# Grouped-query attention on one core: sharing the exponential between ScalarE and VectorE in another pattern, with larger loads

## The chip, the core and the metric

The kernel runs on one core of a Trainium2 chip. The metric is the device time of one execution in microseconds. The engines are named as the profile names them: PE (TensorE matmul; PEld is its weight load), DVE (VectorE), ACT (ScalarE), POOL (GpSimd) and SP (SyncE, which here only issues DMAs). On-chip memory is SBUF; matmuls write PSUM, of which eight banks of 128 x 512 float32 exist in this kernel's tiling.

## What is computed

Eight batches of 512 positions, 32 query heads that share 8 key/value heads in groups of four, 64 values per head. Inputs and output are float32.

```python
batch, seq, n_heads, n_kv_heads, dim = 8, 512, 32, 8, 64
scores = np.einsum('bhqd,bhkd->bhqk', Q, K_expanded) / np.sqrt(dim)
weights = np.exp(scores - np.max(scores, axis=-1, keepdims=True))
weights = weights / (np.sum(weights, axis=-1, keepdims=True) + 1e-10)
output = np.einsum('bhqk,bhkd->bhqd', weights, V_expanded)
```

The order of the 512 keys is free, as long as K and V have the same one: a softmax row sums over all of them.

## The kernel before, in words

The work is cut into 64 jobs; job j is one batch and one key/value head (two jobs make a unit u, eight jobs a batch). A job has four query heads, taken as two head pairs (`i` = 0, 1). Its scores are 16 blocks, each of one head pair, one key chunk `kc` and one head `m` of the pair: 128 keys on the partitions x 512 queries. Each block needs one score matmul, one exponential into `pt` (float16), and its share of the 64 `pv` matmuls (128 x 65: the 65th column of `v` is one, so that the sum of a softmax row comes out beside its values).

Exponentials are made in two ways.

- ACT does two blocks at once: `act_tile` (line 273) has PE write two blocks into a PSUM tile `s_ps` (two buffers of two banks), and ACT reads it and writes `pt` (line 279).
- DVE and POOL do the other blocks of a job by bits: `exp_d` (283) scales the scores to an int16 `u` (290), `exp_d2` (297) takes the low ten bits `f` (301, DVE), makes a factor `g` from it (304, POOL, "the first correction step") and a product `w` (308, POOL), and `exp_d4` (314) adds `w` to `u` (317, DVE), whose bits are the float16 result. `exp_d4` of a job runs in the job behind it.

`WIDE` (line 41) says which jobs give DVE three blocks instead of two: the even jobs from 4 on. A wide job leaves ACT 13 blocks: six tiles of two and one single block, which goes into one bank of the PSUM tile `d_ps` and is made by `act_tile(j, 4, bank)` (called `beside` in the loop). A narrow job leaves ACT 14 blocks, seven tiles. The third block of a wide job is scored and scaled in the job ahead of it (a 128x512 `u`).

Scheduling is by hand: the order of the program is the order on each engine. The loop at line 541 runs the scores and exponentials of job j beside the `pv` matmuls of job j - 1 (`last`). In one turn: tile 0; two score blocks for DVE and their `u`; tile 1; in some jobs a check of V (`check_v`, line 232, DVE); the first 32 `pv` matmuls of `last` in two runs of 16 with tile 2 between them, and `norm` (a reciprocal, line 387, and a product, line 392, both DVE, which read the `pv` tile); tile 3; the single block, if wide; eight transposes of queries for job j + 2 (line 210); `exp_d4(last)`; a check of the sums every eighth job (`check_sums`, line 356, DVE); `exp_d2(j)`; the copy of the transposed queries `qt` (line 214, DVE); then the other 32 `pv` matmuls, cut into three runs by `cut`, with tiles 5 and 6 and the early third block of the next job between them; and `norm` again.

`d_ps` and `pv` have one buffer each of two banks. So the first `pv` matmul of a half waits for the `norm` of the half before it, and new blocks in `d_ps` wait for the `u` and `qt` that read the old ones. In job 61, `norm` also closes the checks (lines 356 and 410 to 413).

Loads are DMAs issued by POOL, which turn float32 into bfloat16 on the way: `load_q` (line 132) one unit of Q, 512 KB as it lands; `load_k` (111) a batch of K; `load_v` (120) a quarter of a batch of V, 128 KB. SP issues the stores and, from `dma_k`, the DMA transposes of K. In the loads `(sc p)` means that a partition holds positions 128 apart.

Of the kernel before, what the change touches and what calls it, by code (L numbers as in the profile page):

```python
# [13 lines left out]
BF16 = mybir.dt.bfloat16  # L14
FP16 = mybir.dt.float16
# [3 lines left out]
ALU = mybir.AluOpType  # L19
# [7 lines left out]
EXP_K = 3.28614867e-04  # L27
EXP_F1 = 1045.05112
# [9 lines left out]
LAST_SUMS = NLAST * 2 * 4  # L38


WIDE = lambda j: j >= 4 and j % 2 == 0


@with_exitstack
# [23 lines left out]
def fast_path(ctx, tc, Q, K, V, out, flag, ident):  # L68
    nc = tc.nc
    B, S, H, D = Q.shape  # L70
    KV = K.shape[2]
    HPG = H // KV
    SC = S // 128
    GP = KV // 2
    NU = B * GP
# [7 lines left out]
    qnat_pool = ctx.enter_context(tc.tile_pool(name="qnat", bufs=4))  # L83
# [20 lines left out]
    vt = [const_pool.tile([128, SC, KV, D + 1], BF16, name=f"v{j}") for j in range(2)]  # L104
# [4 lines left out]
    kn, qn, kt, qt, twice = {}, {}, {}, {}, {}  # L109

    def load_k(b, lo=0, hi=KV):
        if b not in kn:
            kn[b] = knat_pool.tile([128, SC, KV, D], BF16, name="k_nat")
        nc.gpsimd.dma_start(
            out=kn[b][:, :, lo:hi, :],
            in_=K[b, :, lo:hi, :].rearrange("(sc p) g d -> p sc g d", p=128),
        )


    def load_v(b, lo=0, hi=KV, chunks=range(SC)):  # L120
        for sc in chunks:
            nc.gpsimd.dma_start(  # L122
                out=vt[b % 2][:, sc, lo:hi, 0:D],
                in_=V[b, sc * 128:(sc + 1) * 128, lo:hi, :],
            )

    def load_v_head(b, g):
        nc.gpsimd.dma_start(
            out=vt[b % 2][:, :, g, 0:D], in_=V[b, :, g, :].rearrange("(sc p) d -> p sc d", p=128)
        )  # L130

    def load_q(u, lo=0, hi=2 * HPG):
        b, gp = divmod(u, GP)
        h0 = gp * 2 * HPG
        if u not in qn:
            qn[u] = qnat_pool.tile([128, SC, 2 * HPG, D], BF16, name="q_nat")
        nc.gpsimd.dma_start(  # L137
            out=qn[u][:, :, lo:hi, :],
            in_=Q[b, :, h0 + lo:h0 + hi, :].rearrange("(sc p) h d -> p sc h d", p=128),
        )  # L140

# [60 lines left out]
    def trans_q(j, bank, lo=0, hi=NPAIR, other=None):  # L202
        u, g = divmod(j, 2)
        ps = bank.bitcast(BF16).rearrange("p (i sc c) -> p i sc c", i=NPAIR, sc=SC)
        done = []
        for i in range(lo, hi):
            for sc in range(SC):
                h = g * HPG + 2 * i
                done.append(apart(
                    nc.tensor.transpose(ps[:, i, sc, :], qn[u][:, sc, h:h + 2, :], ident), other  # L210
                ))
        if u not in qt:
            qt[u] = qt_pool.tile([128, 2, NPAIR, S], BF16, name="qt")
        return done, lambda: apart(nc.vector.tensor_copy(  # L214
            out=qt[u][:, g, lo:hi, :], in_=ps[:, lo:hi, :, :].rearrange("p i sc c -> p i (sc c)")
        ), other)
# [13 lines left out]
    def check_v(b, sc):  # L230
        n = b * SC + sc
        nc.vector.tensor_reduce(  # L232
            out=okv[:, n:n + 1], in_=vt[b % 2][:, sc, :, 0:D], op=ALU.max, axis=AX.XY,
            apply_absolute_value=True,
        )

    NJOB = NU * 2
    DPAIR = NPAIR - 1  # L240

    def taken(j):
        return 1 if j == NJOB - 1 else 3 if WIDE(j) else 2

# [8 lines left out]
        return [[every[n] for n in group] for group in groups if group]  # L253

    jobs, osb, invs = {}, {}, {}

    def scores(j, ps, i, kc, m):
        u, g = divmod(j, 2)
# [14 lines left out]
    def act_tile(j, n, spare=None):  # L273
        group = act_tiles(j)[n]
        i, kc, lo = group[0]
        ps = s_pool.tile([128, 2, S], FP32, name="s_ps") if spare is None else spare
        for _, _, m in group:
            scores(j, ps[:, m, :], i, kc, m)
        return nc.scalar.activation(  # L279
            out=jobs[j]["pt"][:, i, kc, lo:, :], in_=ps[:, lo:, :], func=EXP, scale=scale  # L280
        )
# [15 lines left out]
    def exp_d2(j, engine=None):  # L297
        st = jobs[j]
        by_bits = engine is None
        engine = engine or nc.gpsimd  # L300
        nc.vector.tensor_single_scalar(  # L301
            out=st["f"], in_=st["u"], scalar=1023, op=ALU.bitwise_and
        )
        engine.tensor_scalar(  # L304
            out=st["g"], in0=st["f"], scalar1=-EXP_F1, scalar2=EXP_K * 2.0 ** (24 * by_bits),
            op0=ALU.add, op1=ALU.mult,
        )
        product = lambda: engine.tensor_tensor(  # L308
            out=st["w"], in0=st["g"], in1=st["f"].bitcast(FP16) if by_bits else st["f"],
            op=ALU.mult,  # L310
        )
        return product() if by_bits else product

    def exp_d4(j):
# [18 lines left out]
    def pv(j, i, lo, hi):  # L333
        st = jobs[j]
        u, g = divmod(j, 2)
        b, gp = divmod(u, GP)
        if lo == 0:

            t = d_tile() if (j, i) == (NJOB - 1, 0) else pv_tile()
            t = t.rearrange("p m (qc c) -> p m qc c", qc=SC)  # L340
            st["pv"][i] = t[:, :, :, 0:D + 1]
        order = blocks(j, i)
        for n in range(lo, hi):
            kc, m, qc = order[n]
            nc.tensor.matmul(  # L345
                st["pv"][i][:, m, qc, :],
                st["pt"][:, i, kc, m, qc * 128:(qc + 1) * 128],
                vt[b % 2][:, kc, 2 * gp + g, :],
                start=(n < 2 * SC and qc == 0),
                stop=(n >= len(order) - 2 * SC and qc == SC - 1),  # L350
            )
# [11 lines left out]
    def check_sums():  # L363
        while full:
            k, n = full.pop()
            cols = n * 2 * SC
            flat = invs.pop(k).rearrange("p s m qc -> p (s m qc)")[:, 0:cols]
            in_bounds((ok[:, 0:cols], ok[:, 0:cols]), flat, ok[:, 0:cols])
# [83 lines left out]
    first_q = Q[0, :, 0:2, :].rearrange("(sc p) h d -> p sc h d", p=128)  # L452

    def key_head(g, queue, part=slice(0, SC)):
        of = K[0, :, g, :].rearrange("(sc p) d -> p sc d", p=128)
        queue.dma_start(out=kf[g][:, part, :], in_=of[:, part, :])

    for queue, part in zip((nc.sync, nc.scalar), parts):
# [8 lines left out]
    for j in range(2):  # L467
        nc.gpsimd.memset(vt[j][:, :, :, D:D + 1], 1.0)
    load_k(0, 2, 4)
    load_q(1)  # L470
    load_v_head(0, 1)
    load_k(0, 4, KV)
    load_v(0, 2, KV)
    nc.gpsimd.memset(ones, 1.0)
    nc.gpsimd.memset(ok, 1.0)

# [17 lines left out]
    for sc in range(SC):  # L494
        n, at = divmod(sc, half)
# [13 lines left out]
    ps = s_tile()  # L509
# [31 lines left out]
    for j in range(1, NJOB - 1):  # L541
        last = j - 1
        u, g = divmod(j, 2)
        b, gp = divmod(u, GP)
        open_job(j)
        if j == 1:

            nc.gpsimd.tensor_copy(out=gate, in_=jobs[0]["pt"][0:1, 0, SC - 1, 0, 0:1])
            load_q(2)
            load_q(3)  # L550
        if g == 0 and u >= 1 and u + 3 < NU:
            load_q(u + 3)
        if (gp, g) == (1, 0) and b + 1 < B:
            load_k(b + 1)
        if 3 <= 2 * gp + g < 3 + SC and b + 1 < B:
            load_v(b + 1, chunks=(2 * gp + g - 3,))
        if j == 1:
            dma_k(0, 2)
        if gp == 2 and g == 0 and b + 1 < B:
            dma_k(b + 1)  # L560

        cut = (4, 18) if taken(j) > 2 else (11, 19)
        act_tile(j, 0)
        if j == 1:
            piece(1, *first_k(1, 0, bank[:, 1, S // 2:]))
        exp_d(j, 0, 2, d_tile())()
        act_tile(j, 1)

        if j == 8:
            check_v(0, 0)  # L570
        if g == 1 and 1 < j and b < B - 1:
            check_v(b, gp)
        if 0 <= j - 8 * (B - 1) < SC:
            check_v(B - 1, j - 8 * (B - 1))
        pv(last, 0, 0, 16)
        act_tile(j, 2)
        pv(last, 0, 16, 32)
        norm(last, 0)
        act_tile(j, 3)

        reads = []
        bank = d_tile()
        beside = act_tile(j, 4, bank) if taken(j) > 2 else None

        ahead = (j + 1,) if j < 2 else (3, 4) if j == 2 else (j + 2,)
        for n, to in enumerate(ahead):
            if to < NJOB:
                reads.append(trans_q(to, bank[:, n, :], other=beside)[1])
        if j == 1:
            reads.append(first_k(1, 1, bank[:, 1, :])[1])  # L590
        exp_d4(last)
        check_sums()
        exp_d2(j)
        copies = [read() for read in reads]
        if taken(j) == 2:
            act_tile(j, 4)
        pv(last, 1, 0, cut[0])
        act_tile(j, 5)
        if taken(j + 1) > 2:
            exp_d(j + 1, 2, taken(j + 1), bank[:, 1:2, :], copies[0])()  # L600
        pv(last, 1, *cut)
        act_tile(j, 6)
        pv(last, 1, cut[1], 32)
        norm(last, 1)
        del jobs[last]
# [146 lines left out]
```

## Time and profile before

| what | value |
| --- | --- |
| time, median of 3 runs | 411.88 us (411.63 to 411.93) |
| time of the profiled execution | 411.81 us |
| its span in the trace | 410.0 us |
| DVE busy | 342.0 us, 608 instructions |
| POOL busy | 306.1 us, 216 instructions |
| DMA packets | 93310, 67.74 MB, mean 165 GB/s |
| HBM read, written | 50.33 MB, 33.55 MB |

A group of instructions is one line of the kernel, one engine and one shape; its row has the busy time, the mean duration of one in ns, and the idle time of the engine ahead of it with what ended that. Timeline rows have the start in us, the duration, and the instruction; neighbours that are alike are merged (x16). Instructions of one engine overlap at their ends: the next one starts before the recorded end of the one ahead of it, so that what an instruction costs in a busy queue is the distance from its start to the next start (or from end to end), which is less than its duration.

### The profile page before, as it was taken

To read this page: it belongs to the slowest core of one execution; us is meant where nothing else is said; L and a number is where in the kernel's file an instruction comes from. 1 tells how busy PE (TensorE), PEld (TensorE's weight loads), DVE (VectorE), ACT (ScalarE), POOL (GpSimd) and SP (SyncE) were. 2 spreads that over 40 slices of the span, in tenths; PEclk is the share of its full clock that TensorE was granted. 3 is DMA by queue.
4 is the path that set the end of the run, shared out by engine and by line. 5 is a ranking of instruction groups with operands and counts; after the bars stand their busy time and mean duration, and the time that the engine had idled before them with its cause. 6 is when DMAs were issued, how large, how long until landed. Compare 5 with 4: busy or idle time off the path is not lost.

```text
span 410.0 us, 13056 instructions
## 1 busy us (share of the span) xinstructions
PE 377.9 (92%) x5670; PEld 233.1 (57%) x5670; DVE 342.0 (83%) x608; ACT 401.2 (98%) x455; POOL 306.1 (75%) x216
## 2 busy tenths in 40 slices
PE   7999999999999999999999999999999999999985
PEld 3565555555555555555655655555555555655553
DVE  4787898888898888888888888888889888998775
ACT  5999999999999999999999999999999999999995
POOL 9868767878679777688777897587776887676562
PEclk9999999999999999999999999999999999999999
DMA  9999984999939995499984999669996799752205
GB/s 145 161 211 190 207 167 134 197 139 198 189 109 227 130 275 116 108 208 127 227 221 79 208 185 213 157 85 213 170 205 156 130 205 199 152 143 104 104 19 195
DMA packets 93310, 67.74 MB, mean 165 GB/s; under 512 B 53312, under 2 KB 76352, under 8 KB 93248
## 3 DMA queue, kind: packets, MB, share of 16 engines
q0 software_dynamic: 55488, 24.91, 52.9%
q1 hardware_dynamic: 37216, 41.75, 36.8%
q8 instruction: 45, 0.74, 0.7%
q10 hardware_dynamic: 544, 0.20, 0.2%
q14 instruction: 17, 0.14, 0.1%
HBM read 50.33 MB, written 33.55 MB: 205 GB/s over the span
## 4 chain that ended last, share of the span: by engine, by line
ACT 79%; PE 12%; DVE 6%; issue 2%; ACTq 0%; DVEq 0%
ACT pt L279 79%; PE s_ps L261 7%; PE pv L345 4%; DVE pt L317 1%; DVE o_sb L392 1%; DVE qt L214 1%; PE s_ps L481 1%; DVE u L290 1%; DVE ok L356 1%; DVE inv L387 0%; PE d_ps L261 0%; DVE f L301 0%; ACTq L279 0%; DVE inv_last L387 0%; PE d_ps L345 0%
## 5 line engine op out<-in xcount | busy, mean ns | idle before, releaser
L279 ACT ACTIVATE pt<-s_ps 128x1024 f16<-128x1024 f32 x418 | 394.7, 1256 | 0.2 <-PE s_ps L261 0.2
L345 PEld LDWEIGHTS <-pt 128*128 128x128 f16 x4096 | 142.1, 98 | 75.7 <-issue 55.6
L345 PE MATMUL pv<-v,pt 128*128 128x65 bf16 x4064 | 179.3, 195 | 1.0 <-DVE o_sb L392 0.7
L261 PE MATMUL s_ps<-qt,kt 64*128 64x512 bf16 x781 | 153.2, 383 | 23.4 <-ACT pt L279 17.0
L308 POOL TENSOR_TENSOR w<-g,f 128x1024 bf16<-128x1024 bf16 (+1 forms) x63 | 163.1, 2588 | 5.3
L304 POOL TENSOR_SCALAR g<-f 128x1024 bf16<-128x1024 int16 (+1 forms) x63 | 78.4, 1244 | 90.6 <-DVE f L301 90.5
L290 DVE TENSOR_SCALAR u<-d_ps 128x1024 int16<-128x1024 f32 (+1 forms) x94 | 97.5, 1037 | 0.0
L261 PEld LDWEIGHTS <-kt 64*128 64x128 bf16 x960 | 55.3, 93 | 66.3 <-issue 37.0
L392 DVE TENSOR_TENSOR o_sb<-pv,inv 128x512 f32<-128x512 f32 x121 | 83.6, 691 | 4.2
L387 DVE RECIPROCAL inv<-pv 128x8 f32<-128x8 f32 x121 | 25.1, 207 | 49.8 <-PE pv L345 49.8
L317 DVE TENSOR_TENSOR pt<-u,w 128x1536 uint16<-128x1536 int16 (+1 forms) x64 | 51.4, 802 | 0.3 <-POOL w L308 0.2
L261 PE MATMUL d_ps<-qt,kt 64*128 64x512 bf16 x179 | 46.1, 375 | 0.1
L214 DVE COPY qt<-d_ps 128x1024 bf16<-128x1024 bf16 x62 | 42.2, 682 | 0.0
L210 PEld LDWEIGHTS <-q_nat 128*128 128x128 bf16 x508 | 28.5, 98 | 20.2 <-issue 20.2
L210 PE MATMUL d_ps<-ident,q_nat 128*128 128x128 bf16 x496 | 38.3, 220 | 0.0
L301 DVE TENSOR_SCALAR f<-u 128x1536 int16<-128x1536 int16 (+1 forms) x64 | 30.7, 480 | 0.0
L122 POOL DMA_DIRECT2D v<-in_V_dram x32 | 29.0, 913 | 0.0
L137 POOL DMA_DIRECT2D q_nat<-in_Q_dram x33 | 27.0, 819 | 0.1
L279 ACT ACTIVATE pt<-d_ps 128x512 f16<-128x512 f32 x30 | 25.9, 863 | 0.0
L232 DVE TENSOR_REDUCE okv<-v 128x1 f32<-128x512 bf16 x32 | 21.6, 675 | 0.0
L261 PE MATMUL s_ps<-qt,kt_first 64*128 64x512 bf16 x56 | 11.1, 399 | 1.7 <-ACT pt L279 1.5
L261 PEld LDWEIGHTS <-kt_first 64*128 64x128 bf16 x64 | 3.9, 94 | 5.6 <-issue 3.0
(57 smaller groups left out, 49.1 us busy)
## 6 DMA issues: line engine op xcount, KB each, us to landing
out_dram<-o_sb SPq DMA_DIRECT2D x31, 1024.0 KB, 7.3
q_nat<-in_Q_dram POOLq DMA_DIRECT2D x31, 512.0 KB, 6.2
k_nat<-in_K_dram POOLq DMA_DIRECT2D x7, 512.0 KB, 8.7
v<-in_V_dram POOLq DMA_DIRECT2D x28, 128.0 KB, 7.4
kt<-kt SPq DMA_DIRECT2D x14, 256.0 KB, 4.4
out_dram<-o_sb SPq DMA_DIRECT2D x4, 256.0 KB, 2.3
kt<-k_nat SPq DMA_TRANSPOSE x32, 6.5
v<-in_V_dram POOLq DMA_DIRECT2D x4, 96.0 KB, 7.6
```

The costliest lines, as they stand in the source:

```text
L122: nc.gpsimd.dma_start(out=vt[b % 2][:, sc, lo:hi, 0:D], in_=V[b, sc * 128:(sc + 1) * 128, lo:hi, :],)
L210: nc.tensor.transpose(ps[:, i, sc, :], qn[u][:, sc, h:h + 2, :], ident), other
L214: return done, lambda: apart(nc.vector.tensor_copy(out=qt[u][:, g, lo:hi, :], in_=ps[:, lo:hi, :, :].rearrange("p i sc c -> p i (sc c)")), ...
L261: return nc.tensor.matmul(ps, keys[64 * m:64 * m + 64, g if u == 0 else g ^ m, kc * 128:(kc + 1) * 128], qt[u][64 * m:64 * m + 64, g, i, : ...
L279: return nc.scalar.activation(out=jobs[j]["pt"][:, i, kc, lo:, :], in_=ps[:, lo:, :], func=EXP, scale=scale)
L290: return lambda: nc.vector.tensor_scalar(out=st["u"][:, lo:hi, :], in0=ps[:, 0:hi - lo, :], scalar1=A_U, scalar2=B_U, op0=ALU.mult, op1=AL ...
L301: nc.vector.tensor_single_scalar(out=st["f"], in_=st["u"], scalar=1023, op=ALU.bitwise_and)
L304: engine.tensor_scalar(out=st["g"], in0=st["f"], scalar1=-EXP_F1, scalar2=EXP_K * 2.0 ** (24 * by_bits), op0=ALU.add, op1=ALU.mult,)
L308: product = lambda: engine.tensor_tensor(out=st["w"], in0=st["g"], in1=st["f"].bitcast(FP16) if by_bits else st["f"], op=ALU.mult,)
L317: nc.vector.tensor_tensor(out=st["pt"][:, DPAIR, :, :, :].rearrange("p kc m q -> p (kc m) q")[:, d_block(j):d_block(j) + n, :].bitcast(U16 ...
L345: nc.tensor.matmul(st["pv"][i][:, m, qc, :], st["pt"][:, i, kc, m, qc * 128:(qc + 1) * 128], vt[b % 2][:, kc, 2 * gp + g, :], start=(n < 2 ...
L392: nc.vector.tensor_tensor(out=osb[u][:, :, h:h + 2, :].rearrange("p qc m d -> p m qc d"), in0=sums[:, :, :, 0:D], in1=inv[:, :, :, None].t ...
```

## The change

`WIDE` becomes three jobs of four: from job 4 on, all but those with j % 4 == 3. In a wide job behind a wide one (j % 4 is 1 or 2) the factor `g` is made by DVE and not by POOL. Where the job behind is wide too (j % 4 is 1), `g` and `w` come later in the program: behind the `u` of the next job's third block. `check_sums` and `check_v` move to between tile 1 and the first `pv` matmuls. In wide jobs the second run of `pv` matmuls moves to before the early block, and `cut` has a third form. K and V are read as `(p sc)`: a partition holds four neighbouring positions. V is loaded a batch at a time, Q two units at a time (the tile has twice the heads), in jobs that a table names.

```diff
-WIDE = lambda j: j >= 4 and j % 2 == 0
+WIDE = lambda j: j >= 4 and j % 4 < 3
...
-    def load_v(b, lo=0, hi=KV, chunks=range(SC)):
-        for sc in chunks:
+    def load_v(b, lo=0):
+        to = vt[b % 2][:, :, lo:, 0:D]
+        of = V[b, :, lo:, :].rearrange("(p sc) g d -> p sc g d", p=128)
+        if lo:
+            for sc in range(SC):
+                nc.gpsimd.dma_start(out=to[:, sc], in_=of[:, sc])
+        else:
             nc.gpsimd.dma_start(
-                out=vt[b % 2][:, sc, lo:hi, 0:D],
-                in_=V[b, sc * 128:(sc + 1) * 128, lo:hi, :],
+                out=to.rearrange("p sc g d -> p (sc g) d"),
+                in_=of.rearrange("p sc g d -> p (sc g) d"),
             )
...
+    def load_q(p, lo=0, hi=4 * HPG):
+        b, at = divmod(p, GP // 2)
+        h0 = at * 4 * HPG
...
+    CHECKS = {}
+    for b in range(B):
+        span = range(max(3, 8 * b + 1), min(8 * b + 9, NJOB - 3))
+        two = [j for j in span if not WIDE(j)]
+        odd = [j for j in span if WIDE(j) and not WIDE(j + 1)]
+        at = [(j, 0) for j in two + odd] + [(j, 1) for j in two]
+        at += [(j, 0) for j in span if j not in two + odd]
+        CHECKS.update(zip(at, [(b, sc) for sc in range(SC)]))
+
+    def in_jobs(load, first, jobs):
+        for n, j in enumerate(jobs):
+            LOADS.setdefault(j, []).append((load, first + n))
+
+    LOADS = {1: [(load_q, 1, 0, 2 * HPG), (load_q, 1, 2 * HPG, 4 * HPG)]}
+    in_jobs(load_k, 1, [3] + [8 * b for b in range(1, B - 1)])
+    in_jobs(load_q, 2, [3, 7, 8] + [8 * b + n for b in range(1, B) for n in (3, 7)][:2 * B - 5])
+    in_jobs(load_v, 1, [8 * b + 4 for b in range(B - 1)])
...
+        odd = WIDE(j) and WIDE(j - 1)
         nc.vector.tensor_single_scalar(
             out=st["f"], in_=st["u"], scalar=1023, op=ALU.bitwise_and
         )
-        engine.tensor_scalar(
-            out=st["g"], in0=st["f"], scalar1=-EXP_F1, scalar2=EXP_K * 2.0 ** (24 * by_bits),
-            op0=ALU.add, op1=ALU.mult,
-        )
...
+        def factor():
+            (nc.vector if odd else engine).tensor_scalar(
+                out=st["g"], in0=st["f"], scalar1=-EXP_F1,
+                scalar2=EXP_K * 2.0 ** (24 * by_bits), op0=ALU.add, op1=ALU.mult,
+            )
...
+        if odd and WIDE(j + 1):
+            return lambda: (factor(), product())
+        factor()
         return product() if by_bits else product
...
-        cut = (4, 18) if taken(j) > 2 else (11, 19)
+        cut = (11, 19) if taken(j) < 3 else (4, 18) if taken(last) < 3 else (4, 16)
...
+        if j < 4 or j % 4 == 0:
+            check_sums()
+        if (j, 0) in CHECKS:
+            check_v(*CHECKS[j, 0])
         pv(last, 0, 0, 16)
...
         exp_d4(last)
-        check_sums()
-        exp_d2(j)
+        rest = exp_d2(j)
...
         act_tile(j, 5)
+        if beside:
+            pv(last, 1, *cut)
         if taken(j + 1) > 2:
             exp_d(j + 1, 2, taken(j + 1), bank[:, 1:2, :], copies[0])()
-        pv(last, 1, *cut)
+        if rest:
+            rest()
+        if (j, 1) in CHECKS:
+            check_v(*CHECKS[j, 1])
+        if not beside:
+            pv(last, 1, *cut)
```

More of the change, by code (lines that the diff above doesn't have):

```diff
@@ L115, in load_k @@
             out=kn[b][:, :, lo:hi, :],
-            in_=K[b, :, lo:hi, :].rearrange("(sc p) g d -> p sc g d", p=128),
+            in_=K[b, :, lo:hi, :].rearrange("(p sc) g d -> p sc g d", p=128),
         )
-    def load_v(b, lo=0, hi=KV, chunks=range(SC)):
-        for sc in chunks:
+    def load_v(b, lo=0):
[5 more added lines that the diff above has]
+        else:
             nc.gpsimd.dma_start(
-                out=vt[b % 2][:, sc, lo:hi, 0:D],
-                in_=V[b, sc * 128:(sc + 1) * 128, lo:hi, :],
+                out=to.rearrange("p sc g d -> p (sc g) d"),
+                in_=of.rearrange("p sc g d -> p (sc g) d"),
             )
@@ L128, in load_v_head @@
         nc.gpsimd.dma_start(
-            out=vt[b % 2][:, :, g, 0:D], in_=V[b, :, g, :].rearrange("(sc p) d -> p sc d", p=128)
+            out=vt[b % 2][:, :, g, 0:D], in_=V[b, :, g, :].rearrange("(p sc) d -> p sc d", p=128)
         )
[L132 to L136, printed above, removed]
+    def load_q(p, lo=0, hi=4 * HPG):
+        b, at = divmod(p, GP // 2)
+        h0 = at * 4 * HPG
+        if p not in qn:
+            qn[p] = qnat_pool.tile([128, SC, 4 * HPG, D], BF16, name="q_nat")
         nc.gpsimd.dma_start(
-            out=qn[u][:, :, lo:hi, :],
+            out=qn[p][:, :, lo:hi, :],
             in_=Q[b, :, h0 + lo:h0 + hi, :].rearrange("(sc p) h d -> p sc h d", p=128),
@@ L207, in trans_q @@
             for sc in range(SC):
-                h = g * HPG + 2 * i
+                h = (u % 2) * 2 * HPG + g * HPG + 2 * i
                 done.append(apart(
-                    nc.tensor.transpose(ps[:, i, sc, :], qn[u][:, sc, h:h + 2, :], ident), other
+                    nc.tensor.transpose(ps[:, i, sc, :], qn[u // 2][:, sc, h:h + 2, :], ident),
+                    other,
                 ))
@@ L303, in exp_d2, with product @@
         )
-        engine.tensor_scalar(
-            out=st["g"], in0=st["f"], scalar1=-EXP_F1, scalar2=EXP_K * 2.0 ** (24 * by_bits),
-            op0=ALU.add, op1=ALU.mult,
-        )
[L308 to L311, printed above, removed]
+        def factor():
[3 more added lines that the diff above has]
+            )
+        def product():
+            engine.tensor_tensor(
+                out=st["w"], in0=st["g"], in1=st["f"].bitcast(FP16) if by_bits else st["f"],
+                op=ALU.mult,
+            )
+        if odd and WIDE(j + 1):
+            return lambda: (factor(), product())
+        factor()
         return product() if by_bits else product
@@ L454, in key_head @@
     def key_head(g, queue, part=slice(0, SC)):
-        of = K[0, :, g, :].rearrange("(sc p) d -> p sc d", p=128)
+        of = K[0, :, g, :].rearrange("(p sc) d -> p sc d", p=128)
         queue.dma_start(out=kf[g][:, part, :], in_=of[:, part, :])
@@ L469, in fast_path @@
     load_k(0, 2, 4)
-    load_q(1)
+    load_k(0, 4, KV)
+    load_q(0, 8, 16)
     load_v_head(0, 1)
-    load_k(0, 4, KV)
-    load_v(0, 2, KV)
+    load_v(0, 2)
     nc.gpsimd.memset(ones, 1.0)
@@ L548, in fast_path @@
             nc.gpsimd.tensor_copy(out=gate, in_=jobs[0]["pt"][0:1, 0, SC - 1, 0, 0:1])
[L549 to L556, printed above, removed]
+        for load, *of in LOADS.get(j, ()):
+            load(*of)
         if j == 1:
@@ L567, in fast_path @@
         act_tile(j, 1)
[L569 to L574, printed above, removed]
+        if j < 4 or j % 4 == 0:
+            check_sums()
+        if (j, 0) in CHECKS:
+            check_v(*CHECKS[j, 0])
         pv(last, 0, 0, 16)
```

## The prediction

> **What bounds the kernel now.** I read the busy times first, then ACT's timeline in the middle of the run, then PE's and DVE's over the same two jobs.
>
> ```profile
> span 410.0 us, 13056 instructions
> PE 377.9 (92%) x5670; PEld 233.1 (57%) x5670; DVE 342.0 (83%) x608; ACT 401.2 (98%) x455; POOL 306.1 (75%) x216
> ```
>
> ACT is busy for 98% of the span. The next fence is its timeline; its last row is the first tile after ACT had waited, from the start of the run.
>
> ```profile
> 209.25 0.91 ACT L279 ACTIVATE pt<-d_ps 128x512 f16<-128x512 f32 x1
> 209.73 12.35 ACT L279 ACTIVATE pt<-s_ps 128x1024 f16<-128x1024 f32 x13
> 221.67 0.90 ACT L279 ACTIVATE pt<-d_ps 128x512 f16<-128x512 f32 x1
> ...
> 9.17 1.02 ACT L279 ACTIVATE pt<-s_ps 128x1024 f16<-128x1024 f32 x1 [0.18 <-PE s_ps L261]
> ```
>
> Rows overlap, so I count from end to end. The single blocks end at 210.16 and 222.57, the 13 tiles between them at 222.08: a tile costs 11.92 / 13 = 0.917 us and a single block 0.49, with no gap. A wide job is 6 x 0.917 + 0.49 = 5.99 us of ACT, a narrow one 6.42. So ACT sets the pace, and a block taken from it is worth 0.917 - 0.49 = 0.427 us while nothing else is late.
>
> How late may something else be? PE, over one wide job (from 205.14) and the start of the next:
>
> ```profile
> 205.14 0.39 PE L261 MATMUL s_ps<-qt,kt 64*128 64x512 bf16 x2
> 206.05 0.39 PE L261 MATMUL s_ps<-qt,kt 64*128 64x512 bf16 x2 [0.31 <-ACT pt L279]
> 206.38 0.67 PE L345 MATMUL pv<-v,pt 128*128 128x65 bf16 x16
> 206.98 0.39 PE L261 MATMUL s_ps<-qt,kt 64*128 64x512 bf16 x2
> 207.30 0.67 PE L345 MATMUL pv<-v,pt 128*128 128x65 bf16 x16
> 207.90 0.39 PE L261 MATMUL s_ps<-qt,kt 64*128 64x512 bf16 x2
> 208.13 0.38 PE L261 MATMUL d_ps<-qt,kt 64*128 64x512 bf16 x1
> 209.23 0.39 PE L261 MATMUL s_ps<-qt,kt 64*128 64x512 bf16 x2
> 210.09 0.39 PE L261 MATMUL s_ps<-qt,kt 64*128 64x512 bf16 x2
> 211.13 0.39 PE L261 MATMUL s_ps<-qt,kt 64*128 64x512 bf16 x2
> 212.04 0.39 PE L261 MATMUL s_ps<-qt,kt 64*128 64x512 bf16 x2 [0.31 <-ACT pt L279]
> 212.37 0.67 PE L345 MATMUL pv<-v,pt 128*128 128x65 bf16 x16
> 212.97 0.39 PE L261 MATMUL s_ps<-qt,kt 64*128 64x512 bf16 x2
> ```
>
> Pairs of score matmuls come 0.92 apart because a tile's buffer is free only when ACT has ended the tile two before it. Sixteen `pv` matmuls fill such a slot (206.38 to 206.98 is 0.60, and 0.33 for the pair), so PE can catch up little: 0.31 in the slot behind the job's first pair. From the free buffer to the end of its tile the least is a hand-over of some 0.06, the pair's 0.39, again 0.06, and 1.02 in ACT, in all 1.53; ACT's pace allows 2 x 0.917 = 1.83. **A pair may be 0.30 us late before ACT stands still**, and what is beyond that is lost for good.
>
> **What the change takes from ACT.** Wide jobs go from 30 (even, 4 to 62) to 45 (three in each four, 4 to 62): 15 x 0.427 = 6.4 us less. PE's work does not change in sum.
>
> **What it puts on DVE.** I call the jobs of a group 4n to 4n+3. DVE's rows in which each instruction starts right behind the other give its costs from start to start:
>
> ```profile
> 208.00 0.21 DVE L387 RECIPROCAL inv<-pv 128x8 f32<-128x8 f32 x1 [0.80 <-PE pv L345]
> 209.46 0.55 DVE L301 TENSOR_SCALAR f<-u 128x1536 int16<-128x1536 int16 x1
> 209.92 0.68 DVE L214 COPY qt<-d_ps 128x1024 bf16<-128x1024 bf16 x1
> 213.03 0.67 DVE L232 TENSOR_REDUCE okv<-v 128x1 f32<-128x512 bf16 x1
> 213.99 0.21 DVE L387 RECIPROCAL inv<-pv 128x8 f32<-128x8 f32 x1 [0.28 <-PE pv L345]
> 214.23 0.69 DVE L392 TENSOR_TENSOR o_sb<-pv,inv 128x512 f32<-128x512 f32 x1
> 214.84 0.95 DVE L317 TENSOR_TENSOR pt<-u,w 128x1536 uint16<-128x1536 int16 x1
> 215.70 0.61 DVE L356 SCALAR_TENSOR_TENSOR ok<-inv,ok 128x128 f32<-128x128 f32 x2
> 217.17 0.68 DVE L290 TENSOR_SCALAR u<-d_ps 128x512 int16<-128x512 f32 x1
> 217.77 0.19 DVE L387 RECIPROCAL inv<-pv 128x8 f32<-128x8 f32 x1
> 218.00 0.69 DVE L392 TENSOR_TENSOR o_sb<-pv,inv 128x512 f32<-128x512 f32 x1
> ```
>
> The new instruction is `g` at 128x1536 on DVE; it ran there once, at 512:
>
> ```profile
> L304 DVE TENSOR_SCALAR g<-f 128x512 bf16<-128x512 int16 x1 | 0.3, 295 | 0.0
> L301 DVE TENSOR_SCALAR f<-u 128x512 int16<-128x512 int16 x1 | 0.3, 287 | 0.0
> L304 POOL TENSOR_SCALAR g<-f 128x1536 bf16<-128x1536 int16 x30 | 44.0, 1467 | 50.0 <-DVE f L301 50.0
> L308 POOL TENSOR_TENSOR w<-g,f 128x1536 bf16<-128x1536 bf16 x30 | 92.9, 3096 | 2.5
> L317 DVE TENSOR_TENSOR pt<-u,w 128x1536 uint16<-128x1536 int16 x30 | 28.5, 949 | 0.2 <-POOL w L308 0.2
> ```
>
> `f` grows from 0.287 at 512 to 0.55 at 1536, so I take 0.56 for `g`, some 0.47 from start to start as `f` has (209.46 to 209.92 is 0.46). Its bounds are 0.30 (the row at 512) and 0.95 (the sum `pt` of the same length); it stands near `f` because the two are 8 ns apart at 512.
>
> Now the chain that matters: the second `norm` of a job frees `pv` for the next job's first run. In 4n+1, from the first reciprocal: reciprocal 0.24, `norm` 0.61, `pt` 0.86, `f` 0.46, `qt` 0.60, `u` of the next job's third block 0.60, `g` 0.47, reciprocal 0.23, `norm` 0.69, hand-over 0.06, in all 4.82. Each part is one of the distances above (`qt` has the length of that `u`). The reciprocal itself waits for PE and comes 2.86 into a wide job (208.00 - 205.14). So `pv` is free 7.68 after the start of 4n+1, which is 1.69 into 4n+2; the first run stands at 1.24 there now (212.37 - 211.13). It is 0.45 late, and so is the pair behind it (212.97 now). Less 0.30, **ACT stands still for 0.15 us in each job 4n+2**. In 14 of the 15 (6 to 58) that is 2.1 us.
>
> In 4n+2 the reciprocal comes at 1.69 + 1.62 = 3.31, `g` needs the whole of `f` right ahead of it (0.55 + 0.03, the gap between 213.99 + 0.21 and 214.23), and there is no third block to scale: 4.34 to the next free `pv`, 0.27 late in 4n+3. That is inside the 0.30, with 0.03 to spare. Jobs 4n+3 (narrow, 6.42) and 4n (no `g`, the narrow 128x1024 `pt`) bring DVE back to where it waits for PE.
>
> The 15th is job 62. Job 61 is narrow now and closes the checks between `norm` and `pt`:
>
> ```profile
> 388.52 0.49 DVE L356 SCALAR_TENSOR_TENSOR ok<-inv,ok 128x72 f32<-128x72 f32 x2
> ...
> 389.44 0.96 DVE L317 TENSOR_TENSOR pt<-u,w 128x1536 uint16<-128x1536 int16 x1
> ...
> 392.08 0.69 DVE L392 TENSOR_TENSOR o_sb<-pv,inv_last 128x512 f32<-128x512 f32 x1
> ```
>
> This adds 0.92 to the chain: 0.45 + 0.92 - 0.30 = 1.07 lost, 1.0 more than now.
>
> **What costs nothing, and under what.** The checks wait where DVE waits for PE: `check_v` takes 0.6 behind a `u`, and 0.28 of waiting was left behind it (213.99); in 4n+2 the `pv` is what is late, so its cover is longer. `check_sums` (0.61) has the 0.80 of a job 4n (208.00). If that cover were gone, they would cost at most 4 x 0.6 + 0.5 a batch, on DVE alone. The early block's score now waits for ACT to have read the single block out of the same bank: that ends at 210.16, so the score can go at 210.22 and the pair behind it at 210.43 rather than 210.09. That pair's tile ends as the pair of the next job at 212.04 gets its buffer, at 211.98; at the least it needs 0.39 + 0.06 + 1.02 = 1.47 before that, so 210.51 would still be in time: 0.08 to spare. The `pv` run that the change moves ahead of that score fills the wait.
>
> POOL loses 30 `g` of 1.47 and the greater part of its load issues, and gains 15 blocks of `w` (a third of 3.10 each). V's issues carry four times the pieces:
>
> ```profile
> L122 POOL DMA_DIRECT2D v<-in_V_dram x32 | 29.0, 913 | 0.0
> L114 POOL DMA_DIRECT2D k_nat<-in_K_dram x9 | 6.8, 757 | 0.0
> ```
>
> A quarter batch of V has 1024 pieces, a load of K 512: 0.156 us for 512 pieces, so a whole batch of V (4096) is an estimated 0.76 + 7 x 0.156 = 1.85 us, with 0.76 and 4 x 0.91 = 3.7 as bounds. It lies in job 8b+4 behind the `w` of a narrow job, where POOL then waits for `f`. The bytes are the same; Q and V are issued at least three jobs (18 us) ahead of their use, and K of batch 1, one job ahead of its DMA transposes, has four jobs until its keys are wanted.
>
> **The sum.** 411.81 (the profiled execution, 1.8 above its span) - 6.4 + 2.1 + 1.0 = 408.5. The execution is 0.07 below the median: **408.5 to 408.6, taken as 408.5 us.**
>
> **Rivals.**
> - *Nothing stands still.* If the slack is 0.15 larger or the chain as much shorter, only job 62 costs: 405.4 to 406.5. For it: 0.45 against 0.30 is a small difference of sums. Against it: DVE's instructions in that chain leave no gap.
> - *DVE costs more, but not all.* The 0.03 to spare in 4n+3 is gone, `g` takes 0.7 rather than 0.56, or a whole-batch load is late once: 0.1 to 0.15 more in two jobs of each group, 3 us: 410 to 411.5.
> - *POOL's product is late: slower.* In 4n+1 `w` can start only behind the late `g`: 2.86 + 0.24 + 0.61 + 0.86 + 0.46 + 0.60 + 0.60 + 0.56 = 6.79, and some 0.1 for the hand-over; with 3.10 it ends 4.0 into 4n+2, where `pt` wants it at 3.31 + 0.85 = 4.16. Each 0.1 beyond that 0.16 makes 4n+3 later and, with 0.03 to spare, costs ACT as much. A group gains 0.43 and loses 0.15, so from 0.45 later than I place it the change is slower; 0.8 later gives 15 x (0.15 + 0.64 - 0.43) + 1.0 = 6.4 more than now, 418. For it: POOL gets the work later in the job. Against it: the `g` that left POOL took half as long as `w`, and `pt` waited 0.2 us for `w` in the whole run.
> - *DVE and POOL shut each other out: slower too.* The `w` of 4n+3 ends some 2.2 into 4n (3.13 for its reciprocal, 0.24 + 0.61 + 0.86 + 0.42 to the end of `f`, 3.3 for POOL's two, less 6.42). If V's issue behind it took 3.7, to 5.9, and kept DVE's `f` (due at 2.86 + 0.85 + 0.60 = 4.3) from starting, `f` would be 1.6 late; less 0.30, and 0.3 in which DVE waits there, ACT loses 1.0 in seven jobs: 415 to 416. Against it: the issue is estimated at half of that, and `f` at 209.46 shows no such wait. By the Trainium skill, "SBUF — State Buffer", Who interferes with whom, a fast two-port `tensor_scalar` of DVE and a GpSimd instruction do lock each other out for a whole instruction; elsewhere the order keeps them apart here, since `pt` ahead of `f` and `g` needs `w`.
>
> **Chances.** The forecast (406.5 to 410) 0.56; nothing stands still 0.2; DVE costs more 0.12; the late product 0.09; the lock 0.03. Within 0.2% (0.8 us, about what a measurement of this kernel can tell from no change) lie 0.02 of the dearer DVE and 0.02 of the late product. So faster 0.86, same 0.04, slower 0.10. The range reaches over the first three, less the third's upper end, and over `g`'s lower bound (0.30, with which no job but 62 stands still); its upper bound of 0.95 would make the chain 0.39 longer and the change slower, and is left out: 405.3 to 411.0.
>
> **What would show it.** ACT's tiles still 0.917 apart but in jobs 4n+2, where the third comes some 0.15 late behind a `pv` run that waits for `norm`; about 1 us in job 62; `g` on DVE at 0.56; 45 single blocks on ACT. The forecast is wrong if ACT has no such gaps, if they stand in other jobs, or if DVE's `pt` waits for `w` for long.

## The result and the profile after

| | before | changed kernel |
| --- | --- | --- |
| median of 6 runs each | 411.90 us (411.61 to 412.64) | 409.56 us (408.94 to 410.13) |
| ratio | | 0.9941, interval 0.9927 to 0.9955 |
| profiled execution | 411.81 us | 410.13 us |
| DVE busy | 342.0 us, 83% | 370.2 us, 91% |

The change saves 2.3 us, where 3.4 were forecast. The page of the changed kernel, span and busy times:

```profile
span 408.3 us, 13010 instructions
PE 374.7 (92%) x5670; PEld 228.2 (56%) x5670; DVE 370.2 (91%) x653; ACT 397.2 (97%) x455; POOL 257.4 (63%) x151
```

ACT is still the busiest engine, but no longer without gaps. The chain of work that ended last, followed back through what released each step, shows it. Its shares of the span, first for the kernel before, then for the changed one:

```profile
ACT 79%; PE 12%; DVE 6%; issue 2%; ACTq 0%; DVEq 0%
```

```profile
DVE 40%; PE 30%; ACT 27%; issue 3%; ACTq 0%; DVEq 0%
```

The groups that the change made, from the changed kernel's groups with their shapes kept apart:

```profile
L301 ACT ACTIVATE pt<-d_ps 128x512 f16<-128x512 f32 x45 | 31.0, 688 | 0.0
L329 DVE TENSOR_SCALAR g<-f 128x1536 bf16<-128x1536 int16 x30 | 16.6, 554 | 0.5
L335 POOL TENSOR_TENSOR w<-g,f 128x1536 bf16<-128x1536 bf16 x45 | 139.2, 3093 | 87.3 <-DVE g L329 86.1
L348 DVE TENSOR_TENSOR pt<-u,w 128x1536 uint16<-128x1536 int16 x45 | 42.6, 947 | 0.0
L127 POOL DMA_DIRECT2D v<-in_V_dram x7 | 12.3, 1759 | 0.0
```

There are 45 single blocks, as counted. `g` takes 0.554 us on DVE (0.56 was estimated), `pt` never waits for `w` (idle before it 0.0), and the issue of a whole batch of V takes 1.76 us on POOL (1.85 estimated).

ACT's timeline over job 42, a job 4n+2:

```profile
263.71 0.77 ACT L301 ACTIVATE pt<-d_ps 128x512 f16<-128x512 f32 x1
264.19 5.94 ACT L301 ACTIVATE pt<-s_ps 128x1024 f16<-128x1024 f32 x6
270.03 0.59 ACT L301 ACTIVATE pt<-d_ps 128x512 f16<-128x512 f32 x1
```

From the end of one single block (264.48) to the end of the sixth tile behind it (270.13) are 5.65 us; six tiles at 0.917 are 5.50. So 0.15 us are missing here. Taken over the whole trace, tile by tile, as the distance from end to end less 0.917 or 0.49, ACT's lost time is 4.75 us, against 0.20 in the kernel before:

| where | lost, us | forecast |
| --- | --- | --- |
| jobs 4n+2 from 6 to 58, at the third tile | 2.0 (14 times 0.13 to 0.17) | 2.1 |
| job 62 | 1.17 | 1.07 |
| first tile of jobs 7, 23, 39 and 55 | 0.63 (0.13 to 0.20 each) | - |
| fourth tile of job 14 | 0.77 | - |
| jobs 2 and 60 | 0.18 | - |

Of the 6.4 us taken from ACT, 6.40 - 4.75 + 0.20 = 1.85 remain by this account; the profiled executions differ by 1.68.

DVE and PE around the start of job 42, from the changed kernel's timeline:

```profile
262.31 0.21 DVE L418 RECIPROCAL inv<-pv 128x8 f32<-128x8 f32 x1 [0.55 <-PE pv L376]
...
265.10 0.68 DVE L312 TENSOR_SCALAR u<-d_ps 128x512 int16<-128x512 f32 x1
265.70 0.55 DVE L329 TENSOR_SCALAR g<-f 128x1536 bf16<-128x1536 int16 x1
266.16 0.20 DVE L418 RECIPROCAL inv<-pv 128x8 f32<-128x8 f32 x1
266.40 0.69 DVE L423 TENSOR_TENSOR o_sb<-pv,inv 128x512 f32<-128x512 f32 x1
```

```profile
264.53 0.37 PE L283 MATMUL d_ps<-qt,kt 64*128 64x512 bf16 x1
...
265.64 0.39 PE L283 MATMUL s_ps<-qt,kt 64*128 64x512 bf16 x2
...
267.14 0.55 PE L376 MATMUL pv<-v,pt 128*128 128x65 bf16 x12 [0.39 <-DVE o_sb L423]
```

The chain is there: reciprocal at 262.31, `g` in it, the `pv` run of job 42 at 267.14, 4.83 us later, and the row says that it waited for DVE's `norm`. The early block's score (264.53) goes 0.05 behind the end of the single block on ACT (264.48), as expected, and costs nothing. Against the end of that single block the `pv` run stands at 2.66 us (267.14 - 264.48); in the kernel before it stands at 2.21 (212.37 - 210.16). So it is 0.45 late, of which ACT loses 0.15.

Job 62, ACT and PE of the changed kernel:

```profile
390.43 1.02 ACT L301 ACTIVATE pt<-s_ps 128x1024 f16<-128x1024 f32 x1 [0.21 <-PE s_ps L283]
392.13 1.95 ACT L301 ACTIVATE pt<-s_ps 128x1024 f16<-128x1024 f32 x2 [0.67 <-PE s_ps L283]
```

```profile
389.79 0.39 PE L283 MATMUL d_ps<-qt,kt 64*128 64x512 bf16 x2 [0.69 <-DVE u L312]
...
391.10 0.67 PE L376 MATMUL pv<-v,pt 128*128 128x65 bf16 x16 [0.70 <-DVE o_sb L423]
```

PE waits for DVE's `u` and then for its `norm`, 0.7 each, and ACT for PE. The wait for `u` costs 0.32 us at the second tile, the wait for `norm` 0.78 at the third.

The losses at the first tile of jobs 7, 23, 39 and 55 are of another kind. PE's two scores and ACT's tile at the start of job 7, in the kernel before:

```profile
49.82 0.39 PE L261 MATMUL s_ps<-qt,kt 64*128 64x512 bf16 x2
50.60 1.02 ACT L279 ACTIVATE pt<-s_ps 128x1024 f16<-128x1024 f32 x1
```

The same in the changed kernel:

```profile
49.76 0.39 PE L283 MATMUL s_ps<-qt,kt 64*128 64x512 bf16 x2
50.55 1.02 ACT L301 ACTIVATE pt<-s_ps 128x1024 f16<-128x1024 f32 x1
```

And for comparison the start of job 11 in the changed kernel:

```profile
74.48 0.39 PE L283 MATMUL s_ps<-qt,kt 64*128 64x512 bf16 x2
75.06 1.06 ACT L301 ACTIVATE pt<-s_ps 128x1024 f16<-128x1024 f32 x1
```

In job 7 ACT starts 0.4 us after its scores are complete, in both kernels; in job 11 of the changed kernel it starts 0.19 after them. Jobs 23, 39 and 55 show 0.36 to 0.37 in both kernels. So PE is not late there: ACT itself starts late, and it did so before the change too. In the kernel before this costs 0.02 or nothing, because ACT's other first tiles (jobs 11, 15, 19) start 0.39 before the recorded end of the tile ahead. In the changed kernel they start only 0.14 before it, and the late start turns into lost time.

### The profile page after: what moved, and what is told of

Same layout as the page of the kernel before. It is cut to its first block, busy times and chain, and to the rows that moved or that the text cites. A ratio compares the mean times of both kernels' runs of the same rounds, so it can differ in the third digit from the quotient of the medians.

```text
span 408.3 us, 13010 instructions
## 1 busy us (share of the span) xinstructions
PE 374.7 (92%) x5670; PEld 228.2 (56%) x5670; DVE 370.2 (91%) x653; ACT 397.2 (97%) x455; POOL 257.4 (63%) x151
## 4 chain that ended last, share of the span: by engine, by line
DVE 40%; PE 30%; ACT 27%; issue 3%; ACTq 0%; DVEq 0%
ACT pt L301 27%; PE pv L376 15%; DVE o_sb L423 11%; PE s_ps L283 11%; DVE u L312 6%; DVE pt L348 6%; DVE qt L220 5%; DVE g L329 4%; DVE inv L418 2%; DVE okv L238 2%; PE d_ps L215 2%; DVE f L324 2%; PE d_ps L283 1%; PE s_ps L512 1%; DVE inv_last L418 0%
## 5 line engine op out<-in xcount | busy, mean ns | idle before, releaser
L301 ACT ACTIVATE pt<-s_ps 128x1024 f16<-128x1024 f32 x403 | 381.3, 1094 | 2.5 <-PE s_ps L283 1.9
L335 POOL TENSOR_TENSOR w<-g,f 128x1536 bf16<-128x1536 bf16 (+1 forms) x63 | 177.4, 2816 | 88.8 <-DVE g L329 86.1
L312 DVE TENSOR_SCALAR u<-d_ps 128x1024 int16<-128x1024 f32 (+1 forms) x109 | 107.8, 989 | 0.3
L283 PEld LDWEIGHTS <-kt 64*128 64x128 bf16 x960 | 50.0, 93 | 53.3 <-issue 29.3
L329 POOL TENSOR_SCALAR g<-f 128x1024 bf16<-128x1024 int16 (+1 forms) x33 | 40.6, 1230 | 53.3 <-DVE f L324 53.3
L283 PE MATMUL d_ps<-qt,kt 64*128 64x512 bf16 x209 | 56.9, 376 | 5.9 <-DVE qt L220 2.3
L301 ACT ACTIVATE pt<-d_ps 128x512 f16<-128x512 f32 x45 | 31.0, 688 | 0.0
L329 DVE TENSOR_SCALAR g<-f 128x1536 bf16<-128x1536 int16 (+1 forms) x31 | 16.9, 546 | 0.6
L142 POOL DMA_DIRECT2D q_nat<-in_Q_dram x19 | 15.4, 812 | 0.1
L127 POOL DMA_DIRECT2D v<-in_V_dram x7 | 12.3, 1759 | 0.0
```

What stands on the lines that cost most here:

```text
L283: return nc.tensor.matmul(ps, keys[64 * m:64 * m + 64, g if u == 0 else g ^ m, kc * 128:(kc + 1) * 128], qt[u][64 * m:64 * m + 64, g, i, : ...
L301: return nc.scalar.activation(out=jobs[j]["pt"][:, i, kc, lo:, :], in_=ps[:, lo:, :], func=EXP, scale=scale)
L312: return lambda: nc.vector.tensor_scalar(out=st["u"][:, lo:hi, :], in0=ps[:, 0:hi - lo, :], scalar1=A_U, scalar2=B_U, op0=ALU.mult, op1=AL ...
L329: (nc.vector if odd else engine).tensor_scalar(out=st["g"], in0=st["f"], scalar1=-EXP_F1, scalar2=EXP_K * 2.0 ** (24 * by_bits), op0=ALU.a ...
L335: engine.tensor_tensor(out=st["w"], in0=st["g"], in1=st["f"].bitcast(FP16) if by_bits else st["f"], op=ALU.mult,)
```

## The experiments

All are edits of the changed kernel, and all compute the whole reference. Ratios are to the kernel before, run on the same chip. Some of those runs reach 413 to 416 us (the medians are 411.99 and 411.86), and the ratios come out up to 0.004 lower than those of the medians.

### The factor on POOL everywhere

```diff
-        odd = WIDE(j) and WIDE(j - 1)
+        odd = False
```

> The changed kernel with the factor g on POOL in all jobs, straight behind f. Theory (VectorE's chain in job 4n+1 is too long by the 0.47 us of g): the first pv run of 4n+2 comes 0.45 us earlier, ACT's loss of 0.14 us there goes (2.0 us over 14 jobs), the losses of 0.13 to 0.2 us in jobs 7, 23, 39 and 55 shrink with it, and the time falls by 2 to 2.8 us to about 407 us; w ends about 3.85 us into 4n+2, so that pt waits there 0.1 to 0.2 us for it, and some 0.25 us in 4n+3, which costs nothing. Rival 1 (PE is overfull in wide jobs, or held by the early block's wait for ACT): the loss in 4n+2 stays, the time stays at 409.5 us. Rival 2 (POOL needed the relief): pt waits for w by 0.5 us or more in 4n+2 and 4n+3, and the time is 410 us or more.

Measured: 406.77 us (406.66 to 407.5, 5 runs), ratio 0.985 (0.9811 to 0.989). Its ACT, DVE and PE around the start of job 42:

```profile
261.98 0.77 ACT L301 ACTIVATE pt<-d_ps 128x512 f16<-128x512 f32 x1
262.45 5.79 ACT L301 ACTIVATE pt<-s_ps 128x1024 f16<-128x1024 f32 x6
```

```profile
260.57 0.21 DVE L418 RECIPROCAL inv<-pv 128x8 f32<-128x8 f32 x1 [0.54 <-PE pv L376]
...
263.36 0.68 DVE L312 TENSOR_SCALAR u<-d_ps 128x512 int16<-128x512 f32 x1
264.01 0.21 DVE L418 RECIPROCAL inv<-pv 128x8 f32<-128x8 f32 x1
264.25 0.69 DVE L423 TENSOR_TENSOR o_sb<-pv,inv 128x512 f32<-128x512 f32 x1
```

```profile
263.91 0.39 PE L283 MATMUL s_ps<-qt,kt 64*128 64x512 bf16 x2
...
265.00 0.67 PE L376 MATMUL pv<-v,pt 128*128 128x65 bf16 x16
```

The six tiles end 5.49 after the single block (262.75 to 268.24): nothing is lost. From the reciprocal to the `pv` run are 4.43 us, not 4.83, and the run no longer waits for `norm`. All fourteen losses in 4n+2 are gone; in job 7, 0.02 is lost instead of 0.16, and in 23, 39 and 55 nothing. Among the waits the largest new row is:

```profile
DVE pt L348 <- POOL w L335: 5.2, 15, 0.7
```

`pt` waits 15 times for `w`, 0.35 us in the mean, all in the jobs 4n+3. Up to job 55 it costs ACT nothing; behind the one in job 59 (0.32), 0.11 is lost at the third tile of job 60. In 4n+2 it waits 0.04 to 0.11 us, less than expected. Only one wait, in job 63, is longer than 0.5. Both rivals are out.

### The factor on POOL in one of the two jobs

In 4n+1 alone:

```diff
+        odd = WIDE(j) and WIDE(j - 1) and not WIDE(j + 1)
```

> The changed kernel with g back on POOL in jobs 4n+1 alone; in 4n+2 it stays on VectorE. Theory: as with g on POOL everywhere, since only the chain of 4n+1 was too long: no loss of ACT in 4n+2, 407 us; pt in 4n+3 does not wait for w. Rival 1 (PE overfull): 409.5 us. Rival 2 (POOL needed the relief in 4n+1): pt of 4n+2 waits 0.5 us or more, 410 us or more.

Measured: 408.12 us (406.19 to 408.71, 5 runs), ratio 0.9867 (0.9826 to 0.9909). In its profiled execution (408.71, the slowest) the losses in 4n+2 are gone but for stalls of PE in jobs 14 and 30 (0.97 and 0.71, below); 55 and 62 lose 0.30 and 0.68. So `g` on DVE in 4n+2 costs nothing by the trace; the time is above the 407 that was expected by about such a stall.

In 4n+2 alone:

```diff
+        odd = WIDE(j) and WIDE(j - 1) and WIDE(j + 1)
```

> The changed kernel with g on POOL in jobs 4n+2 alone; in 4n+1 it stays on VectorE, behind the third block's u. Theory (only the chain of 4n+1 is too long): ACT still loses 0.14 us in each job 4n+2, and the time stays at 409.3 to 409.8 us; w of 4n+2 comes later, and pt in 4n+3 waits for it 0.2 to 0.4 us. Rival (any g on VectorE costs, and each of the two jobs has its half of the loss): losses of 0.05 to 0.1 us, 408 to 408.5 us.

Measured: 410.58 us (410.2 to 411.42, 7 runs), ratio 0.9956 (0.9922 to 0.999), 0.8 above the upper end of what was expected. The losses of the changed kernel are there but for the stall in job 14, 0.13 to 0.18 in the jobs 4n+2 up to 54 and 0.33 in 58. ACT in job 42:

```profile
262.90 0.77 ACT L301 ACTIVATE pt<-d_ps 128x512 f16<-128x512 f32 x1
263.38 5.94 ACT L301 ACTIVATE pt<-s_ps 128x1024 f16<-128x1024 f32 x6
```

The six tiles end 5.65 after the single block, as in the changed kernel. The two runs together put the whole of this loss on `g` in 4n+1. The median is a microsecond above the changed kernel's, and the accounts of the profiled executions show some 0.6 of it: 4.61 us are lost here, and 4.75 - 0.77 = 3.98 in the changed kernel without its stall in job 14. Job 58 loses 0.33, and 0.31 is lost at the third tile of job 60, where the changed kernel loses nothing. In the jobs 4n+3 `pt` waits 0.51 us in the mean for `w`, where 0.2 to 0.4 were expected. In job 59, ahead of the loss in job 60, it waits 0.52; with `g` on POOL everywhere it was a wait of 0.32 and a loss of 0.11, 0.20 less of each. The rest of the microsecond stays open.

### The checks closed earlier

```diff
-NLAST = 7
+NLAST = 9
```

> The changed kernel with the checks closed in job 60 instead of job 61 (NLAST 9). Theory (the chain of VectorE in job 61, lengthened by 0.92 us of closing checks, holds up job 62): ACT's loss in job 62 falls from 1.17 us to about 0.15 us, the 0.92 us lie in job 60 where VectorE waits for PE, and the time falls by 0.9 to 1.0 us, to about 408.6 us (ratio to the kernel before 0.992). Rival (the end is set by the last products and stores, and ACT's loss in job 62 would come back there): no change, 409.5 us.

Measured: 409.18 us (408.93 to 410.3, 7 runs), ratio 0.9916 (0.9884 to 0.9948): not told apart from the changed kernel. The loss in job 62 fell to 0.70, but 0.52 appeared in job 61: over jobs 60 to 62, 1.31 instead of 1.25. The expectation (1.0 us less) was wrong about job 60: a wide job ahead of a wide one has no 0.9 us to spare on DVE, and the closing checks only moved the lateness one job ahead.

### Job 61 narrow, the factor on POOL

```diff
-WIDE = lambda j: j >= 4 and j % 4 < 3
+WIDE = lambda j: j >= 4 and j % 4 < 3 and j != 61
...
-        odd = WIDE(j) and WIDE(j - 1)
+        odd = False
```

> The changed kernel with g on POOL in all jobs and job 61 narrow, so that no wide job follows it closely. Theory (in job 61 the closing checks and the chain of a wide job add up; a wide job 61 gains 0.43 us and loses 1.1 us in jobs 60 to 63): those losses fall to 0.1 to 0.2 us, ACT works 0.43 us more, and the time is 0.5 to 0.7 us below that of g on POOL alone (406.8 us), some 406.2 us. Rival (the losses at the end come from the last products and not from job 61): 407.2 us.

Measured: 406.64 us (406.56 to 407.02, 4 runs), ratio 0.987 (0.9847 to 0.9893). Job 62 loses 0.03 instead of 0.70, but 60 and 61 lose 0.52 and 0.20, so that only 0.37 of the 1.1 came back, about what ACT's additional 0.43 us of work takes. So the 0.5 to 0.7 us that were expected did not come: it is not told apart from the factor on POOL alone. These two are the best of the versions, 5.2 us below the kernel before (by the medians on their chips) and 2.8 to 2.9 below the changed one.

### V in quarters

```diff
-    in_jobs(load_v, 1, [8 * b + 4 for b in range(B - 1)])
+    for b in range(B - 1):
+        for sc in range(SC):
+            LOADS.setdefault(8 * b + 3 + sc, []).append((load_v, b + 1, 0, (sc,)))
```

> The changed kernel with V loaded a quarter of a batch at a time again, in jobs 8b+3 to 8b+6; all else as changed. Theory (the whole-batch burst of V, 4096 small pieces, delays the fetch of PE's instructions, and the one stall of 0.7 us in job 14 came from that): no stall of PE on its own issue above 0.3 us, the gaps between the fetches of PE's instructions stay under 12 us, the time falls by 0.3 to 0.8 us to about 409 us and its runs lie closer together. Rival (the stall was chance and has nothing to do with V): the time stays at 409.5 us and stalls of 0.5 us or more appear in other jobs. Either way ACT still loses 0.14 us in each job 4n+2.

This was about the 0.77 us in job 14. PE's timeline of the changed kernel there:

```profile
95.03 0.39 PE L283 MATMUL s_ps<-qt,kt 64*128 64x512 bf16 x2
96.13 0.65 PE L376 MATMUL pv<-v,pt 128*128 128x65 bf16 x16 [0.71 <-issue]
```

"issue" says that PE waited for nothing that the trace shows. The records of the instruction queue, in blocks of 16 KB at a time, some 9 us apart, show a gap ahead of it, from 78.2 to 93.0. The quarters gave 409.9 us (409.67 to 410.7, 11 runs), ratio 0.9936 (0.9913 to 0.996): not faster, and the expectation failed. In the profiled execution the stall was gone and the gap was 12.1 us, but so they were with whole batches where `g` was on POOL (gap 8.6), and in the run with `g` on POOL in 4n+2 alone (8.8). In the three executions with the stall in job 14 (changed kernel, early checks, `g` on POOL in 4n+1) the gap was 14.1 to 14.8. At that place late instructions as the cause would fit all of these. But gaps as long stand elsewhere without a stall: 14.1 us from 318.5 in the changed kernel, 14.0 from 121.2 with the quarters. So the length of the gap alone does not make a stall, and the cause is not shown. V's burst alone does not bring it.

### Everything but the pattern

```diff
-WIDE = lambda j: j >= 4 and j % 4 < 3
+WIDE = lambda j: j >= 4 and j % 2 == 0
```

> The changed kernel with the old pattern of wide jobs (even jobs); loads, layouts, the places of the checks and the program order as changed. Theory (ACT had no gap that these could close, and they are hidden): as the kernel before, within 0.4 us. Rival 1 (loads and checks give part of the gain): 411.2 us or less. Rival 2 (the larger loads cost time, by waits of PE for the first queries or for its instructions): 412.5 us or more.

Measured: 412.16 us (411.83 to 412.47, 10 runs), ratio 1.0002 (0.9987 to 1.0016). The loads, the layouts and the places of the checks are worth nothing by themselves with the old pattern: ACT had no gap to close, and loses 0.22 us here as it lost 0.20.

### The low bits in VectorE's wait

With `g` on POOL, `f` of 4n+1 ahead of the first `pv` matmuls:

```diff
+        if WIDE(j) and j % 4 == 1:
+            low_bits(j)
+            jobs[j]["early"] = True
         pv(last, 0, 0, 16)
```

> The changed kernel with g on POOL in all jobs, and f of the jobs 4n+1 moved ahead of the first reciprocal, into the 0.5 to 0.7 us in which VectorE waits for PE. POOL's w of 4n is still running there, until some 3.5 us into the job. By the lock that the Trainium skill states (SBUF - State Buffer, Who interferes with whom), f, in VectorE's fast form, starts only when w has ended: f takes or waits 1 us or more, norm comes 1 us late, and ACT loses some 0.5 to 0.9 us in each of 15 jobs: 414 to 420 us. Without a lock: f takes 0.55 us as ever, VectorE's chain is 0.46 us shorter, and the time stays at 406.8 us, since nothing is late there any more.

Measured: 426.25 us (426.06 and 426.45), ratio 1.0343 (1.0312 to 1.0374). DVE and POOL in job 37:

```profile
243.03 1.69 DVE L321 TENSOR_SCALAR f<-u 128x1536 int16<-128x1536 int16 x1
...
245.48 1.60 DVE L353 TENSOR_TENSOR pt<-u,w 128x1536 uint16<-128x1536 int16 x1
```

```profile
241.21 3.09 POOL L340 TENSOR_TENSOR w<-g,f 128x1536 bf16<-128x1536 bf16 x1
244.81 1.47 POOL L334 TENSOR_SCALAR g<-f 128x1536 bf16<-128x1536 int16 x1 [0.50 <-DVE f L321]
246.36 3.67 POOL L340 TENSOR_TENSOR w<-g,f 128x1536 bf16<-128x1536 bf16 x1
```

`f` comes while `w` runs (to 244.30) and takes 1.69 us instead of 0.55: it ends 0.42 behind `w`. Then `pt` comes while POOL makes `g` (to 246.28) and takes 1.60 instead of 0.95. ACT loses 0.77 in each job 4n+1, 0.18 in 4n+2, and 5.5 in job 62. This is the lock that "SBUF — State Buffer", Who interferes with whom, of the Trainium skill states for a two-port `tensor_scalar` and for a `tensor_tensor` with both inputs in SBUF. The trace agrees, with 1.69 and 1.60 us.

The time is 6 us above the upper end of what was expected. The losses in the 15 jobs are in the range given (0.5 to 0.9), but the expectation had no term for job 62. There it is the closing checks, DVE and POOL in job 61:

```profile
398.35 4.05 DVE L392 SCALAR_TENSOR_TENSOR ok<-inv,ok 128x72 f32<-128x72 f32 x2
```

```profile
399.23 3.08 POOL L340 TENSOR_TENSOR w<-g,f 128x1536 bf16<-128x1536 bf16 x1
```

These two instructions took 0.49 us in the kernel before and in the changed one. Here `g` (397.68 to 399.15) and `w` (to 402.31) run beside them, and they end at 402.40, 0.09 behind `w`. PE then waits 3.74 us for the `pt` behind the checks, and ACT's next tile, the first of job 62, 4.36 us for PE.

## Why the prediction came out as it did

- **What bounds the kernel, and what a block is worth.** Right. 45 single blocks, no gap on ACT where nothing else is late, and where `g` is on POOL most of the 6.4 us arrives: 411.99 to 406.77 on one chip, 5.2, with 1.1 lost in jobs 60 to 63.
- **The chain of 4n+1.** Right in place, cause and size: 4.82 us forecast, 4.83 measured; 2.1 us forecast as lost, 2.0 measured. Taking `g` out of 4n+1 removed the loss in both runs that did it, and taking it out of 4n+2 did not.
- **The 0.30 us of slack.** Right within the 0.02 that the losses show (0.13 to 0.17, where 0.15 was forecast). The lateness of 0.45 is found as well, against the end of ACT's single block.
- **Job 62.** Right in size: 1.07 forecast, 1.17 measured, and gone (0.03) where job 61 was narrow. The forecast named the wait for `norm` alone; 0.32 of it is lost a tile earlier, where PE waits for `u` because `d_ps` has one buffer.
- **What costs nothing.** Right for the loads, the layouts and the checks together (ratio 1.0002, measured with the old pattern), for the early block and for the late product. The estimate of V's issue was 5% high.
- **4n+3 with 0.03 to spare.** Right: at the third tile of the jobs 4n+3, which this was about, ACT loses nothing in any of them.
- **Not in the sum: the first tile of jobs 7, 23, 39 and 55,** 0.63 us together. The forecast took it that a tile is late only when its scores are. Here the scores were complete 0.4 us before. The late start is in the kernel before too, where it was hidden; the forecast did not ask what else ACT's reserve was hiding. Where `g` of 4n+1 was on POOL, the tiles at the start of most jobs 4n+3 start 0.27 before the recorded end of the tile ahead, not 0.14, and these four lose 0.02 or nothing (55 lost 0.30 in one of the two runs, behind a stall of PE). Two such starts are 128 recorded instructions of ACT apart (112 tiles and 16 waits). What delays them was not tried.
- **Not in the sum either:** the 0.77 in job 14, a wait of PE for no engine. It is not in every execution, and the runs of the changed kernel spread over 1.2 us. The profiled execution is 1.63 us above the forecast, and these two losses are 1.40 of it.
- **What the forecast did not ask:** whether `g` had to leave POOL. It took from its own numbers that `w` behind the DVE's `g` would end 4.0 us into the next job. With `g` on POOL straight behind `f`, the `w` of job 41 ends 4.83 us behind the end of its single block on ACT, with `g` on DVE 4.93: not later at all, and DVE has one instruction less in the chain that counts. That part of the change cost 2.8 us (409.56 to 406.77, with 411.90 and 411.99 for the kernel before beside them), and the rest of it gave more than the whole.

## What to carry to other kernels

When work is moved to an engine with spare time in the mean, price the chain between its two releases of a buffer that has no second copy: there an added instruction counts in full, and the rest of the engine's idle time does not help. Measure beforehand how late that release may be (here 0.30 us). Ask of each part of a change by itself what it is for: here the instruction that went to the busier engine undid more than half of what the rest gained.

## What the runs showed of the hardware

DVE and POOL shutting each other out was allowed for, not expected at this price: one `f`, moved ahead of three instructions of DVE, made the kernel 20 us slower than its own base (406.77 to 426.25). It hit three kinds of DVE's instructions: `f` (1.69 us instead of 0.55), `pt` (1.60 instead of 0.95) and the two closing checks (4.05 instead of 0.49). POOL's `w` was longer too, 3.67 us where it met DVE, against 3.09. In the other kernels `pt`, `f` and `g` find no `g` or `w` running on POOL, because `pt` needs `w` and POOL's next work needs `f`. So the idle time of POOL (37% of the span in the changed kernel) is not simply free for DVE to use.

A wait at the start can also be seen: with `g` on POOL, PE waited in job 2 for queries.

```profile
22.84 0.62 PE L215 MATMUL d_ps<-ident,q_nat 128*128 128x128 bf16 x8 [0.81 <-DMA q_nat<-in_Q_dram]
```

ACT's loss in that job was 0.10, 0.29, 0.39, 0.59 or 1.09 us in the profiled executions of the changed kernel and its edits, whose first loads are all the same. Part of the spread of the runs may come from there; this was not followed from run to run.
